# The order of VectorE's side work in a streamed-weight decoder layer: sums, prepared blocks and low parts issued behind the weights' low parts

## The chip, the cores and the metric

One core of a Trainium2 chip. The metric is device time in microseconds (us) of one launch; lower is better. In the profile PE is TensorE, DVE VectorE, ACT ScalarE, POOL GpSimd and SP SyncE, which issues nearly all transfers.

## The reference

One decoder layer on x of 256 tokens and 2048 channels, in float32: three residual blocks, each behind an RMSNorm, and a last RMSNorm.

```python
def swiglu(x, w_gate, w_up, w_down):
    return (jax.nn.silu(x @ w_gate) * (x @ w_up)) @ w_down

x = x + 0.5 * swiglu(rmsnorm(x), ...)                 # D_FF 5632
x = x + mixer(rmsnorm(x))                             # w_in: q,k,v,u,v_sg and two gates, 2048 wide each
x = x + 0.5 * swiglu(rmsnorm(x), ...)
out = rmsnorm(x)
```

The mixer projects once by `w_in`, runs dilated causal attention and a spatial gating unit beside each other, projects both to 2048 channels, merges them by sigmoid gates of `w_in`'s last columns and projects the merge by `w_out`.

## The kernel before

**Weights.** With 256 tokens all weights are used once, so they are streamed. A *unit* is a weight block of 2 x 128 rows by 512 columns. SyncE loads it into one of five buffers `raw` (`load_unit`, L206). Products must keep float32 accuracy, so each block is split: ScalarE rounds it to the high part `wh` (L281), VectorE subtracts for the low part `wl` (L282). Both live in a ring of nine slots of 128 rows. TensorE then makes three products for each slot and each of two token tiles, high x high, high x low and low x high (L288). One such ordinary step ("n") has twelve matmuls. The activations are split likewise: `xhi`/`xlo` for the block's normed input, `hA`/`hB` for the FFN's inner product (L380, L381).

**Quads.** Two neighbouring column groups of a product share a 2 x 2 arrangement of weight blocks (b11, b21, b12, b22) that is multiplied with seven products in place of eight (Strassen's method in Winograd's form). The products, `p1` to `p7`, are steps of their own ("s") of two or three slots, nine matmuls in a quad of three. VectorE prepares their weights from the blocks: t2 = b12 - b11, t1 = t2 - b22, t4 = b21 - t2 and, where the transfer doesn't add them up, b12 + b22 (`prepare`, L257 and L260). In the FFNs b12 + b22 is made by a second, accumulating load, which GpSimd issues once SyncE's load of b12 has landed (L247). VectorE also makes four sums of the activation blocks (`sums_of`, L360 to L363), which are split again into `fx`/`fh`. p1, p6 and p7 run among the last steps of the group before ("opening"), p5, p4, p3 and p2 among the first steps of their own ("closing": 1, 2, 4 and 6 ordinary steps in, where there are more than nine of them). Between them the partial results are copied or added between banks: after p1 and p7 a copy on ScalarE (L338, L343), after p6 one into `part` (L341), after p7 VectorE takes p7's result off `part` (L345), and after p5 it writes q12, a sum of p5's bank and `part` (L347), on which p3 then accumulates. A quad's blocks are loaded again for the next quad as they come free; the first quad of each home (FFN 1, gates, FFN 2) is loaded by `move_in`.

**Order.** The program is written out step by step, and each engine runs its instructions in the order in which they are written. For each step: its matmuls (`products`), then all callbacks that are due (a heap with due times counted in steps), then `advance`, which loads units and writes the splits of steps further on, three steps and up to two more if the ring has room. Quads' blocks are prepared at fixed steps beside p6: b12 + b22 three before, t2 two before, t1 two behind, t4 five behind, each just ahead of that step's split. So VectorE's and ScalarE's queues hold, between weight splits, the readings of banks directly behind the product, sums and low parts of activations when their callbacks come due, and prepared blocks at their fixed steps.

**Norms.** After each residual add (L471) ScalarE squares the sum (L437), VectorE and GpSimd make the reciprocal root (L441, L442, L444), and x is transposed through memory: VectorE writes `btx` (L408), SyncE stores it as `bmx` (L392) and reads it back as `xt` (L398), and some steps later (`lag`) ScalarE scales it by the gains (L490) and it is split. The FFN's product goes the same way.

Of the kernel before, what the change touches and what calls it, by code (L numbers as in the profile page):

```python
# [10 lines left out]
F32 = mybir.dt.float32  # L11
# [13 lines left out]
NC = 512  # L25
# [20 lines left out]
MORE = 7  # L46
UK = 4


@with_exitstack  # L50
def layer(ctx: ExitStack, tc: tile.TileContext, a, out):
    nc = tc.nc
    PE, ACT, DVE, POOL, SP = nc.tensor, nc.scalar, nc.vector, nc.gpsimd, nc.sync
    big = ctx.enter_context(tc.tile_pool(name="big", bufs=1))
# [54 lines left out]
    quads = []  # L109
    prepared = {}  # L110
    ends = []
# [16 lines left out]
    def lay_out():  # L128
        i, count = 0, 0
        while i < len(gemms):  # L130
            g = gemms[i]
            size, stage = g["group"]
            quad = g["quad"]
            taken = range(quad["k0"] // 2, quad["k0"] // 2 + quad["nq"]) if quad else ()
            order = [(p, q) for p in range(size) for q in range(gemms[i + p]["nk"] // 2) if q not in taken]
            if stage:
                order.sort(key=lambda s: stage(*s, gemms[i + s[0]]["nk"] // 2))
            new = [("n", (gemms[i + p], q // 2, q % 2)) for p, q in order]
            if quad:
                nq = quad["nq"]  # L140
                quad["gemms"] = gemms[i], gemms[i + 1]
                for k, form in opening(count):
# [42 lines left out]
    def at(i, fn):  # L185
        heapq.heappush(callbacks, (i, next(counter), fn))

    def start_of(w):
# [53 lines left out]
    def load_block(quad, b):  # L242
        if quad is None:
            return
        SP.dma_start(blocks_of(quad)[b], block(quad, b))
        if b == 2 and quad["home"] in homes:
            POOL.dma_start(blocks_of(quad)[b], block(quad, 3), accum_op=OP.add)  # L247
# [5 lines left out]
    def prepare(quad, what):  # L253
        b11, b21, b12, b22, t2, t1, _ = blocks_of(quad)
        if what == "t3":
            if quad["home"] not in homes:
                DVE.tensor_tensor(b12, b12, b22, op=OP.add)  # L257
            return
        out, x, y = {"t1": (t1, t2, b22), "t2": (t2, b12, b11), "t4": (t2, b21, t2)}[what]
        DVE.tensor_tensor(out, x, y, op=OP.subtract)  # L260

# [8 lines left out]

    now = [0.0]

    def split(i, k=None):
        for quad, what in prepared.pop(i, []):
            prepare(quad, what)
        kind, s = steps[i]
        r = raws[place[i]] if kind == "n" else form_of(*s)
        for first, end in runs(i, k or range(len(slots[i]))):
            o = slots[i][first]
            wh, wl = (v[:, o:o + end - first] for v in ring)  # L280
            ACT.activation(wh, r[:, first:end], AF.Copy)  # L281
            DVE.tensor_tensor(wl, r[:, first:end], wh.bitcast(F32), op=OP.subtract)  # L282
        if kind == "s" and s[1] in FREES:
            at(now[0] + 2, lambda: load_block(next_of(s[0]), FREES[s[1]]))

# [32 lines left out]
    def quad_products(i, quad, form):  # L318
# [17 lines left out]
        part = blocks_of(quad)[-1]  # L336
        if form == "p1":
            ACT.activation(q11, x_, AF.Copy)  # L338
            first["begun"][0] = True
        elif form == "p6":  # L340
            ACT.activation(part, x_, AF.Copy)  # L341
        elif form == "p7":
            ACT.activation(q21, x_, AF.Copy)  # L343
            first["begun"][1] = True
            DVE.tensor_tensor(part, part, x_, op=OP.subtract)  # L345
        elif form == "p5":
            DVE.tensor_tensor(q12, x_, part, op=OP.add)  # L347
            second["begun"][0] = True
        close(g, i)

    def sums_of(i, keep, q0, nq, store, v, name, tag="gate"):

        got = {}

        def sums():
# [6 lines left out]
            DVE.tensor_tensor(s3, a1, a0, op=OP.subtract)  # L362
            DVE.tensor_tensor(s4, b0, s2, op=OP.subtract)  # L363

        def parts():
            keep["both"] = both = store()
            split_psum(*both, got["f"])
# [10 lines left out]

    def split_psum(hi, lo, src):
        ACT.activation(hi, src, AF.Copy)  # L380
        DVE.tensor_tensor(lo, src, hi.bitcast(F32), op=OP.subtract)  # L381

# [83 lines left out]
    def residual(e, n, c, banks, scale, norm):  # L466
        cs = slice(c * NC, (c + 1) * NC)

        def add():
# [3 lines left out]
            if norm:  # L473
                if c == 0:
                    norm_open(n)
                norm_squares(n, c)

        at(e + 1, add)
        if not norm:
            return  # L480
        if c == 3:
            at(e + 2, lambda: norm_rstd(n))

        turn_x(e + (6 if c == 1 else 2), n, c, 6)

    def turn_x(i, n, c, lag, read=3):
        def evac(src):
# [3 lines left out]
            hi, lo = (turned(xT[p][:, 4 * c:4 * c + 4]) for p in ("hi", "lo"))  # L491
            split_psum(hi, lo, src)
            tag = "gate" if n == 1 else "tmp"
# [14 lines left out]
    def ffn(wg, wu, wd, down_post, group):  # L508
# [10 lines left out]
        for after, (part, quads_of) in zip(GATES, enumerate(PARTS)):  # L519
            for f in range(*after):  # L520
# [13 lines left out]
                def post_up(e, banks, st=st, f=f, kl=kl, quads_here=quads_here):  # L534
# [11 lines left out]
                    def ev(src):  # L546
                        hi, lo = (v[:, kl:kl + 4] for v in home["h"])
                        split_psum(turned(hi), turned(lo), src)
                        if first == 0:
                            st["fs"] = sb.tile([P, 2, 4, 3, P], F32R, tag="L", name=f"fh{e}")  # L550
                            sums_of(e + 10, st, 0, 2, lambda: [st["fs"][:, h, :, 0:2] for h in range(2)], src, f"h{e}")
                        elif first == 1 and quads_here["nq"] == 3:
                            sums_of(e + 10, st, 2, 1, lambda: [st["fs"][:, h, :, 2:3] for h in range(2)], src, f"h{e}")

# [598 lines left out]
    for i in range(n):  # L1153
# [10 lines left out]
        if i > 0:  # L1164
            advance(i)
    for t in range(NT):
        known(t)
# [52 lines left out]
```

## Time and profile before

| | us |
|---|---|
| three runs | 2029.78, 2031.58, 2035.73; median 2031.58 |
| the profiled execution | 2030.45 |
| its span | 2028.7 |
| TensorE busy | 1987.0 (98%) |
| VectorE busy | 1585.5 (78%) |
| ScalarE busy | 1177.8 (58%) |

The profile lists, for each engine, how long it waited, for which other engine's instruction and how often; the timeline shows single instructions with start, duration and, in brackets, the idle time ahead of them and what ended it. The first FFN runs from the start to about 670 us, the mixer from there to about 1360, the second FFN to the end.

### The profile page before, as it was taken

To read this page: it belongs to the slowest core of one execution; us is meant where nothing else is said; L and a number is where in the kernel's file an instruction comes from. 1 tells how busy PE (TensorE), PEld (TensorE's weight loads), DVE (VectorE), ACT (ScalarE), POOL (GpSimd) and SP (SyncE) were. 2 spreads that over 40 slices of the span, in tenths; PEclk is the share of its full clock that TensorE was granted. 3 is DMA by queue.
4 is the path that set the end of the run, shared out by engine and by line. 5 is a ranking of instruction groups with operands and counts; after the bars stand their busy time and mean duration, and the time that the engine had idled before them with its cause. 6 is when DMAs were issued, how large, how long until landed. Compare 5 with 4: busy or idle time off the path is not lost.

```text
span 2028.7 us, 25057 instructions
## 1 busy us (share of the span) xinstructions
PE 1987.0 (98%) x9188; PEld 1723.7 (85%) x9188; DVE 1585.5 (78%) x1652; ACT 1177.8 (58%) x1381; POOL 51.4 (3%) x50
## 2 busy tenths in 40 slices
PE   9999999999999999999999999989999999999998
PEld 8878888888888878888888888878888888888887
DVE  6788888887897689676665777787888878888876
ACT  7565555665665566455454555565665565655564
POOL 0000000000000000000000000000000000000000
PEclk9999999999999999999999999999999999999999
DMA  9888878877777985888887766788778877888783
GB/s 318 264 239 264 257 231 243 274 229 250 246 234 231 279 268 180 232 291 254 264 242 242 216 206 219 221 260 246 242 233 263 254 231 235 252 240 253 241 271 125
DMA packets 265445, 493.91 MB, mean 243 GB/s; under 512 B 17517, under 2 KB 46057, under 8 KB 265193
## 3 DMA queue, kind: packets, MB, share of 16 engines
q1 hardware_dynamic: 253624, 469.49, 71.9%
q0 software_dynamic: 11376, 22.28, 6.2%
q8 instruction: 72, 1.18, 0.2%
q10 hardware_dynamic: 320, 0.53, 0.1%
q14 instruction: 53, 0.43, 0.1%
HBM read 462.58 MB, written 29.66 MB: 243 GB/s over the span
## 4 chain that ended last, share of the span: by engine, by line
PE 75%; DVE 10%; DMA 6%; issue 4%; ACT 3%; SPq 1%; DVEq 0%; ACTq 0%; POOLq 0%; POOL 0%
PE qd L288 52%; PE mm L288 22%; DVE wl L282 6%; DMA xt<-bmx 2%; ACT wh L281 1%; DMA raw<-in_ffn_w_gate_dram 1%; DVE quads L260 1%; SPq L398 1%; DMA bmx<-btx 1%; DMA quads<-in_ffn_w_gate_dram 1%; ACT xt L490 1%; DVE sum L260 0%; DVE hB L381 0%; ACT xhi L380 0%; DVE btx L408 0%
## 5 line engine op out<-in xcount | busy, mean ns | idle before, releaser
L282 DVE TENSOR_TENSOR wl<-raw,wh 128x1024 fp32r<-128x1024 f32 (+1 forms) x638 | 695.4, 1107 | 202.1 <-ACT wh L281 200.7
L281 ACT ACTIVATE wh<-raw 128x1024 fp32r<-128x1024 f32 (+1 forms) x638 | 599.6, 961 | 312.2 <-PE qd L288 152.5
L288 PE MATMUL qd<-wl,xhi 128*128 128x512 f32 x1201 | 457.7, 381 | 8.9 <-DVE wl L282 8.9
L288 PE MATMUL qd<-wh,xhi 128*128 128x512 f32 x1201 | 456.7, 380 | 3.8 <-ACT wh L281 3.8
L288 PE MATMUL qd<-wh,xlo 128*128 128x512 f32 x1201 | 456.7, 380 | 0.0
L282 DVE TENSOR_TENSOR wl<-quads,wh 128x1536 fp32r<-128x1536 f32 (+2 forms) x223 | 290.9, 1317 | 94.4 <-ACT wh L281 93.1
L281 ACT ACTIVATE wh<-quads 128x1536 fp32r<-128x1536 f32 (+2 forms) x223 | 249.0, 1127 | 174.6 <-PE qd L288 153.2
L288 PEld LDWEIGHTS qd<-wl,xhi 128*128 128x128 f32 x1201 | 227.6, 190 | 44.7 <-DVE wl L282 12.4
L288 PEld LDWEIGHTS qd<-wh,xhi 128*128 128x128 f32 x1201 | 227.6, 189 | 37.4 <-ACT wh L281 5.0
L288 PEld LDWEIGHTS qd<-wh,xlo 128*128 128x128 f32 x1201 | 227.8, 190 | 32.2
L288 PE MATMUL mm<-wh,xhi 128*128 128x512 f32 x608 | 231.7, 381 | 0.4 <-ACT xhi L380 0.2
L288 PE MATMUL mm<-wh,xlo 128*128 128x512 f32 x608 | 230.9, 380 | 0.6 <-DVE xlo L381 0.6
L288 PE MATMUL mm<-wl,xhi 128*128 128x512 f32 x608 | 229.4, 380 | 0.1
L288 PE MATMUL qd<-wl,hA 128*128 128x512 f32 x564 | 214.1, 380 | 1.8 <-DVE wl L282 1.8
L288 PE MATMUL qd<-wh,hA 128*128 128x512 f32 x564 | 213.8, 379 | 0.0
L288 PE MATMUL qd<-wh,hB 128*128 128x512 f32 x564 | 213.8, 379 | 0.0
L282 DVE TENSOR_TENSOR wl<-sum,wh 128x1024 fp32r<-128x1024 f32 (+2 forms) x85 | 117.8, 1393 | 64.0 <-ACT wh L281 64.0
L288 PEld LDWEIGHTS mm<-wl,xhi 128*128 128x128 f32 x608 | 115.2, 189 | 18.0 <-DVE wl L282 1.9
L288 PEld LDWEIGHTS mm<-wh,xlo 128*128 128x128 f32 x608 | 115.2, 189 | 17.4 <-DVE xlo L381 1.0
L288 PEld LDWEIGHTS mm<-wh,xhi 128*128 128x128 f32 x608 | 115.2, 189 | 17.1 <-ACT xhi L380 0.6
L288 PE MATMUL qd<-wh,fx 128*128 128x512 f32 x352 | 120.2, 382 | 4.3 <-ACT wh L281 4.0
L281 ACT ACTIVATE wh<-sum 128x1024 fp32r<-128x1024 f32 (+2 forms) x85 | 100.7, 1191 | 38.3 <-PE qd L288 26.6
(453 smaller groups left out, 2192.1 us busy)
## 6 DMA issues: line engine op xcount, KB each, us to landing
raw<-in_w_in_dram SPq DMA_DIRECT2D x168, 512.0 KB, 4.8
raw<-in_ffn_w_down_dram SPq DMA_DIRECT2D x120, 512.0 KB, 5.0
raw<-in_ffn_w_up_dram SPq DMA_DIRECT2D x112, 512.0 KB, 6.1
raw<-in_ffn_w_gate_dram SPq DMA_DIRECT2D x111, 512.0 KB, 4.1
quads<-in_ffn_w_gate_dram SPq DMA_DIRECT2D x38, 768.0 KB, 5.3
quads<-in_ffn_w_up_dram SPq DMA_DIRECT2D x38, 768.0 KB, 5.9
quads<-in_ffn_w_down_dram SPq DMA_DIRECT2D x32, 512.0 KB, 6.0
quads<-in_ffn_w_up_dram POOLq DMA_DIRECT2D x19, 768.0 KB, 11.1
```

Of the source, the lines that this page charges most:

```text
L260: DVE.tensor_tensor(out, x, y, op=OP.subtract)
L281: ACT.activation(wh, r[:, first:end], AF.Copy)
L282: DVE.tensor_tensor(wl, r[:, first:end], wh.bitcast(F32), op=OP.subtract)
L288: PE.matmul(g["ps"][t], act, in_turn(w), start=not g["begun"][t], stop=g["left"][t] == 0, skip_group_check=g["quad"] is not None)
L398: SP.dma_start(e[32 * j:32 * j + 32].rearrange("p (i r) -> p i r", i=4), m[j])
L490: ACT.activation(v, v, AF.Copy, scale=g)
```

## The change

- `Metered` stands in for VectorE when instructions are written. It books 0.03 us plus a microsecond per 950 columns for each in `load`; at each step's end `work_off` takes 2.6 off per ordinary step.
- Low parts of activations and the four sums may be handed to `extra` with a slack. `work_off` writes them at the end of a step, behind its weight splits, if they are ready and `load` with them stays within 2.9, or if their slack has run out. hB gets 4 steps, the sums of h 5, those of x 1; xlo of mixer and second FFN comes one step later, except the last block's. The sums' split follows two steps behind the sums (one for x) and not one.
- Quads' blocks are no longer prepared at fixed steps. `prepare_ready` takes the next (b12 + b22, t2, t1, t4) at a step's end if the blocks' loads were issued three steps ago or more, the product that still needs the old contents has been split, and `load` allows; `prepare_for` writes it at the latest ahead of the split that uses it.
- Readings of banks (p1, p6, p7, p5) are gathered in `after_splits` and written behind the step's splits.
- The closing order is p5, p3, p4, p2 at 1, 2, 3 and 5 ordinary steps (short groups: 1, 2, 3, 4).
- The block that p5 frees is loaded one step later and not two; squares are made three steps behind the add and not one, the root four and not two; the last transposed block is scaled seven steps after its transpose and not six; the first blocks of the gates' and the second FFN's quads are loaded 4 and 2 steps later.

No instruction is added or removed on TensorE, VectorE, ScalarE or SyncE; some instructions only change place. The core of the diff:

```diff
+TICK = 2.6
+FULL = 2.9
+class Metered:
+        def call(out, *args, **kwargs):
...
+            self.load += 0.03 + columns / 950
+            return method(out, *args, **kwargs)
...
     def closing(count):
-        return zip((1, 2, 4, 6) if count > 9 else (1, 2, 3, 5), ("p5", "p4", "p3", "p2"))
+        return zip((1, 2, 3, 5) if count > 9 else (1, 2, 3, 4), ("p5", "p3", "p4", "p2"))
...
+    def work_off():
+        DVE.load = max(0.0, DVE.load - TICK * (now[0] - now[1]))
+        now[1] = now[0]
+        while True:
+            ready = [e for e in extras if e[2] <= now[0]]
+            if not ready:
+                return
+            e = min(ready)
+            if e[0] > now[0] and DVE.load + e[3] > FULL:
+                return
...
+            e[4]()
...
+    NEEDS = {"f": ((2, 3), ()), "t2": ((0, 2), ("p1",)), "t1": ((3,), ("p1",)), "t4": ((1,), ("p6",))}
+    USES = {"p6": "t2", "p7": "f", "p5": "t1", "p4": "t4"}
+    def prepare_ready():
...
+            if (all(quad["loaded"].get(b, 1e9) + 3 <= now[0] for b in blocks) and quad["split"].issuperset(forms)
+                    and DVE.load + 0.56 * quad["nq"] * (NC / 512) <= FULL):
...
+                prepare_next(quad)
...
-            at(now[0] + 2, lambda: load_block(next_of(s[0]), FREES[s[1]]))
+            at(now[0] + (1 if s[1] == "p5" else 2), lambda: load_block(next_of(s[0]), FREES[s[1]]))
...
+        after_splits.append(read)
...
-        at(i, sums)
-        at(i + 1, parts)
+        at(i + 1, lambda: extra(0, slack, 0.6 + 0.6 * nq, sums) if slack > 1 else sums())
...
+        if slack:
+            extra(1, slack, 1.1, rest)
+        else:
+            rest()
...
-        turn_x(e + (6 if c == 1 else 2), n, c, 6)
+        at(e + 3, lambda: norm_squares(n, c))
         if c == 3:
-            at(e + 2, lambda: norm_rstd(n))
+            at(e + 4, lambda: norm_rstd(n))
+        turn_x(e + (6 if c == 1 else 2), n, c, 7 if c == 3 else 6)
...
-    for after, home in ((16, homes[0]), (mixer + 1, gates), (start_of(ffn2_gate) + 1, homes[1])):
+    for after, home in ((16, homes[0]), (mixer + 5, gates), (start_of(ffn2_gate) + 3, homes[1])):
...
-    for i, (kind, s) in enumerate(steps):
-        if kind == "s" and s[1] == "p6":
-            for k, what in ((-3, "t3"), (-2, "t2"), (2, "t1"), (5, "t4")):
-                prepared.setdefault(i + k, []).append((s[0], what))
...
         if i > 0:
             advance(i)
+        for fn in after_splits:
+            fn()
+        after_splits.clear()
+        work_off()
+        prepare_ready()
```

How it moves the instructions, at three places. First VectorE around p5 of the first FFN's first quad (97 to 108 us in the trace). `sg` is the gate's activation times the up product, `fsh` the four sums of h, `fh` their split, `wl<-sum` and `wl<-quads` low parts of a quad's block, `qd_2` the q12 sum. Before:

```order
L381 TENSOR_TENSOR hB<-sg19.0_583,hA 128x1024
L360 TENSOR_TENSOR fsh23.0_847<-sg19.0_583 128x256
L361 TENSOR_TENSOR fsh23.0_847<-sg19.0_583,fsh23.0_847 128x256
L362 TENSOR_TENSOR fsh23.0_847<-sg19.0_583 128x256
L363 TENSOR_TENSOR fsh23.0_847<-sg19.0_583,fsh23.0_847 128x256
L381 TENSOR_TENSOR fh23.0_846<-fsh23.0_847,fh23.0_846 128x4x256
L543 SCALAR_TENSOR_TENSOR sg27.75_738<-mm_0_291,rstd_443,sg27.75_738 128x512
L543 SCALAR_TENSOR_TENSOR sg27.75_738<-mm_1_292,rstd_443,sg27.75_738 128x512
L282 TENSOR_TENSOR wl<-sum,wh 128x512
L282 TENSOR_TENSOR wl<-sum,wh 128x1024
L347 TENSOR_TENSOR qd_2_706<-qd_3_707,quads 128x512
L282 TENSOR_TENSOR wl<-raw_739,wh 128x1024
```

After (all VectorE instructions bear L66, the line in `Metered`):

```order
L66 SCALAR_TENSOR_TENSOR sg27.75_740<-mm_0_291,rstd_440,sg27.75_740 128x512
L66 SCALAR_TENSOR_TENSOR sg27.75_740<-mm_1_292,rstd_440,sg27.75_740 128x512
L66 TENSOR_TENSOR wl<-quads,wh 128x512
L66 TENSOR_TENSOR wl<-quads,wh 128x1024
L66 TENSOR_TENSOR hB<-sg19.0_583,hA 128x1024
L66 TENSOR_TENSOR wl<-raw_741,wh 128x1024
L66 TENSOR_TENSOR qd_2_707<-qd_3_708,quads 128x512
L66 TENSOR_TENSOR fsh23.0_880<-sg19.0_583 128x256
L66 TENSOR_TENSOR fsh23.0_880<-sg19.0_583,fsh23.0_880 128x256
L66 TENSOR_TENSOR fsh23.0_880<-sg19.0_583 128x256
L66 TENSOR_TENSOR fsh23.0_880<-sg19.0_583,fsh23.0_880 128x256
```

hB and the sums went behind a quad's low part, the sums behind the q12 sum as well, the q12 sum behind one more `wl<-raw`, and the low part ahead of it is now p3's (`quads`) and no longer p4's (`sum`). fh's split stands five low parts further down.

Second, SyncE at the start of the second FFN (1352 to 1370 us). Before:

```order
L206 DMA raw_9768<-in_ffn_w_up_dram 128x2x512
L245 DMA quads<-in_ffn_w_gate_dram 128x3x512
L245 DMA quads<-in_ffn_w_up_dram 128x3x512 x2
L245 DMA quads<-in_ffn_w_gate_dram 128x3x512
L206 DMA raw_9813<-in_ffn_w_up_dram 128x2x512
L392 DMA bmx_3_9837<-btx_3_9834 128x1024
```

After:

```order
L250 DMA raw_9764<-in_ffn_w_up_dram 128x2x512
L250 DMA raw_9795<-in_ffn_w_up_dram 128x2x512
L468 DMA bmx_3_9815<-btx_3_9812 128x1024
L290 DMA quads<-in_ffn_w_gate_dram 128x3x512
L290 DMA quads<-in_ffn_w_up_dram 128x3x512 x2
L290 DMA quads<-in_ffn_w_gate_dram 128x3x512
```

The four loads of the first quad stand behind one unit and behind the store of the last transposed block.

Third, VectorE at the same place (1371 to 1388 us): `wl<-quads` is p1's low part, `sum<-quads` t2, `quads<-sum,quads` t1, `wl<-sum` p6's low part. Before:

```order
L282 TENSOR_TENSOR wl<-quads,wh 128x1536
L260 TENSOR_TENSOR sum<-quads 128x1536
L282 TENSOR_TENSOR wl<-raw_9813,wh 128x512 x2
L381 TENSOR_TENSOR xlo_9404<-xt_3_9881,xhi_9403 128x1024
L282 TENSOR_TENSOR wl<-raw_9839,wh 128x1024
L282 TENSOR_TENSOR wl<-sum,wh 128x1536
```

After:

```order
L66 TENSOR_TENSOR wl<-quads,wh 128x1536
L66 TENSOR_TENSOR sum<-quads 128x1536
L66 TENSOR_TENSOR wl<-raw_9795,wh 128x512 x2
L66 TENSOR_TENSOR wl<-raw_9838,wh 128x1024
L66 TENSOR_TENSOR quads<-sum,quads 128x1536
L66 TENSOR_TENSOR xlo_9400<-xt_3_9885,xhi_9399 128x1024
L66 TENSOR_TENSOR wl<-sum,wh 128x1536
```

t2 keeps its place behind p1's low part; t1 has come ahead of p6's, and the last xlo went behind one more low part and t1.

More of the change, by code (lines that the diff above doesn't have):

```diff
@@ L47, with __init__, __getattr__ @@
 UK = 4
+TICK = 2.6
+FULL = 2.9
+class Metered:
+    def __init__(self, engine):
+        self.engine, self.load = engine, 0.0
+    def __getattr__(self, name):
+        method = getattr(self.engine, name)
+        def call(out, *args, **kwargs):
+            columns = 1
+            for n in out.shape[1:]:
+                columns *= n
+            self.load += 0.03 + columns / 950
+            return method(out, *args, **kwargs)
+        return call
 @with_exitstack
@@ L52, in layer @@
     nc = tc.nc
-    PE, ACT, DVE, POOL, SP = nc.tensor, nc.scalar, nc.vector, nc.gpsimd, nc.sync
+    PE, ACT, DVE, POOL, SP = nc.tensor, nc.scalar, Metered(nc.vector), nc.gpsimd, nc.sync
     big = ctx.enter_context(tc.tile_pool(name="big", bufs=1))
@@ L109, in layer @@
     quads = []
-    prepared = {}
     ends = []
@@ L141, in lay_out @@
                 quad["gemms"] = gemms[i], gemms[i + 1]
+                quad["loaded"], quad["split"] = {}, set()
+                quad["todo"] = ["t2", "t1", "t4"] if quad["home"] in homes else ["f", "t2", "t1", "t4"]
                 for k, form in opening(count):
@@ L186, in at, with extra @@
         heapq.heappush(callbacks, (i, next(counter), fn))
+    now = [0.0, 0.0]
+    extras = []
+    after_splits = []
+    def extra(wait, slack, cost, fn):
+        heapq.heappush(extras, (now[0] + slack, next(counter), now[0] + wait, cost, fn))
+    def work_off():
[8 more added lines that the diff above has]
+                return
+            extras.remove(e)
+            heapq.heapify(extras)
+            e[4]()
     def start_of(w):
@@ L244, in load_block @@
             return
+        quad["loaded"][b] = now[0]
         SP.dma_start(blocks_of(quad)[b], block(quad, b))
@@ L254, in prepare, with prepare_next, prepare_for @@
         b11, b21, b12, b22, t2, t1, _ = blocks_of(quad)
[L255 to L260, printed above, removed]
+        out, x, y, op = {"f": (b12, b12, b22, OP.add), "t1": (t1, t2, b22, OP.subtract),
+                         "t2": (t2, b12, b11, OP.subtract), "t4": (t2, b21, t2, OP.subtract)}[what]
+        DVE.tensor_tensor(out, x, y, op=op)
+    NEEDS = {"f": ((2, 3), ()), "t2": ((0, 2), ("p1",)), "t1": ((3,), ("p1",)), "t4": ((1,), ("p6",))}
+    USES = {"p6": "t2", "p7": "f", "p5": "t1", "p4": "t4"}
+    def prepare_next(quad):
+        prepare(quad, quad["todo"].pop(0))
+    def prepare_ready():
+        for quad in started:
+            if not quad["todo"]:
+                continue
+            what = quad["todo"][0]
+            blocks, forms = NEEDS[what]
+            if (all(quad["loaded"].get(b, 1e9) + 3 <= now[0] for b in blocks) and quad["split"].issuperset(forms)
+                    and DVE.load + 0.56 * quad["nq"] * (NC / 512) <= FULL):
+                assert all(b in quad["loaded"] for b in blocks)
+                prepare_next(quad)
+    def prepare_for(quad, form):
+        while USES.get(form) in quad["todo"]:
+            assert all(b in quad["loaded"] for b in NEEDS[quad["todo"][0]][0]), (form, quad["todo"])
+            prepare_next(quad)
+    started = []
     def form_of(quad, form):
@@ L269, in layer @@
     ring = [big.tile([P, RING, NC], F32R, name=name) for name in ("wh", "wl")]
-    now = [0.0]
     def split(i, k=None):
-        for quad, what in prepared.pop(i, []):
-            prepare(quad, what)
         kind, s = steps[i]
+        if kind == "s":
+            if s[1] == "p1":
+                started.append(s[0])
+            prepare_for(*s)
+            s[0]["split"].add(s[1])
         r = raws[place[i]] if kind == "n" else form_of(*s)
@@ L336, in quad_products, with read, sums_of @@
         part = blocks_of(quad)[-1]
[L337 to L348, printed above, removed]
+        def read():
+            if form == "p1":
+                ACT.activation(q11, x_, AF.Copy)
+            elif form == "p6":
+                ACT.activation(part, x_, AF.Copy)
+            elif form == "p7":
+                ACT.activation(q21, x_, AF.Copy)
+                DVE.tensor_tensor(part, part, x_, op=OP.subtract)
+            elif form == "p5":
+                DVE.tensor_tensor(q12, x_, part, op=OP.add)
+        after_splits.append(read)
+        if form in ("p1", "p7", "p5"):
+            (second if form == "p5" else first)["begun"][form == "p7"] = True
         close(g, i)
-    def sums_of(i, keep, q0, nq, store, v, name, tag="gate"):
+    def sums_of(i, keep, q0, nq, store, v, name, tag="gate", slack=1):
         got = {}
@@ L363, in sums @@
             DVE.tensor_tensor(s4, b0, s2, op=OP.subtract)
+            at(now[0] + min(2, slack), parts)
         def parts():
             keep["both"] = both = store()
-            split_psum(*both, got["f"])
+            split_psum(*both, got["f"], slack // 2)
             keep.setdefault("forms", {}).update({q0 + q: [v[:, :, q] for v in both] for q in range(nq)})
-        at(i, sums)
-        at(i + 1, parts)
+        at(i + 1, lambda: extra(0, slack, 0.6 + 0.6 * nq, sums) if slack > 1 else sums())
     def forms_tile(pool, tag, name, nq):
@@ L491, in evac @@
             hi, lo = (turned(xT[p][:, 4 * c:4 * c + 4]) for p in ("hi", "lo"))
-            split_psum(hi, lo, src)
+            split_psum(hi, lo, src, 1 if n and c < 3 else 0)
             tag = "gate" if n == 1 else "tmp"
@@ L547, in ev @@
                         hi, lo = (v[:, kl:kl + 4] for v in home["h"])
[L548 removed]
+                        split_psum(turned(hi), turned(lo), src, 0 if last else 4)
                         if first == 0:
                             st["fs"] = sb.tile([P, 2, 4, 3, P], F32R, tag="L", name=f"fh{e}")
[L551 removed]
+                            sums_of(e + 10, st, 0, 2, lambda: [st["fs"][:, h, :, 0:2] for h in range(2)], src, f"h{e}", slack=5)
                         elif first == 1 and quads_here["nq"] == 3:
[L553 removed]
+                            sums_of(e + 10, st, 2, 1, lambda: [st["fs"][:, h, :, 2:3] for h in range(2)], src, f"h{e}", slack=5)
                     at(e + 1, mul)
```

6 lines of the change are left out of this document (3 added, 3 removed).

## The prediction

> **What bounds the kernel now.** I read the page first, then TensorE's waits, the same waits by window, and the timelines around the longest of them. The page:
>
> ```profile
> span 2028.7 us, 25057 instructions
> PE 1987.0 (98%) x9188; PEld 1723.7 (85%) x9188; DVE 1585.5 (78%) x1652; ACT 1177.8 (58%) x1381; POOL 51.4 (3%) x50
> ```
>
> TensorE bounds it: it is busy 1987.0 of 2028.7 us, and the change leaves its work as it is. Only its stops can be won. TensorE's waits over the whole span, the two rows that matter (sum, times, longest):
>
> ```profile
> PE qd L288 <- DVE wl L282: 22.9, 26, 2.1
> PE qd L288 <- ACT wh L281: 7.7, 10, 1.8
> ```
>
> 36 stops, 30.6 us, all for the low or high part of a weight block. Where they lie: the same view for 20 to 640 us (first FFN), 640 to 720 (its end and the mixer's start), 1280 to 1400 (the mixer's end and the second FFN's start) and 1400 to 2020 (second FFN), in this order:
>
> ```profile
> PE qd L288 <- DVE wl L282: 6.4, 7, 1.9
> PE qd L288 <- ACT wh L281: 1.4, 3, 0.8
> ```
> ```profile
> PE qd L288 <- DVE wl L282: 3.9, 4, 2.1
> PE qd L288 <- ACT wh L281: 1.2, 1, 1.2
> ```
> ```profile
> PE qd L288 <- DVE wl L282: 6.6, 8, 1.7
> PE qd L288 <- ACT wh L281: 2.6, 2, 1.8
> ```
> ```profile
> PE qd L288 <- DVE wl L282: 5.3, 6, 1.3
> PE qd L288 <- ACT wh L281: 2.5, 4, 1.2
> ```
>
> A stop costs more than its idle time. TensorE's timeline at the longest of the first FFN (six rows left out between 107.12 and 110.19):
>
> ```profile
> 103.67 0.38 PE L288 MATMUL qd<-wh,xhi 128*128 128x512 f32 x1
> 105.98 0.48 PE L288 MATMUL qd<-wl,xhi 128*128 128x512 f32 x1 [1.93 <-DVE wl L282]
> ...
> 107.12 0.72 PE L288 MATMUL qd<-wl,xhi 128*128 128x512 f32 x1 [0.22 <-DVE wl L282]
> ...
> 110.19 0.60 PE L288 MATMUL qd<-wh,xlo 128*128 128x512 f32 x1
> 110.62 0.39 PE L288 MATMUL qd<-wh,xhi 128*128 128x512 f32 x1
> ```
>
> And TensorE undisturbed (one row left out between the first two), at the end of a product p5, with VectorE's work on that bank behind it:
>
> ```profile
> 1145.55 0.38 PE L288 MATMUL qd<-wh,uTB 128*128 128x512 f32 x1
> ...
> 1145.99 0.38 PE L288 MATMUL qd<-wh,uTA 128*128 128x512 f32 x1
> 1146.20 0.38 PE L288 MATMUL qd<-wh,xhi 128*128 128x512 f32 x1
> ```
> ```profile
> 1147.37 0.70 DVE L347 TENSOR_TENSOR qd<-qd,part 128x512 f32<-128x512 f32 x1
> 1147.97 1.22 DVE L282 TENSOR_TENSOR wl<-raw,wh 128x1024 fp32r<-128x1024 f32 x1
> ```
>
> Starts lie 0.65/3 = 0.217 us apart, so twelve matmuls, one ordinary step, take 2.60 us. A stop loses the overlap of the last matmul's end (0.38 - 0.217 = 0.16) and makes the next one longer (0.48 for 0.38): 0.26 beside its idle time. From 107.12 to 110.62 eight matmuls take 3.50 us where 1.73 are usual: a clock drop, 1.77 lost. I count three such drops: here, at 715 (one matmul's row below) and behind the stop at 1384, shown further down. Everything that the stops cost is 30.6 idle + 36 x 0.26 (9.4) + 3 x 1.77 (5.3) = 45 us.
>
> What VectorE did ahead of the stop at 105.98, in its timeline (from the start of an activation's low part to the weights' that TensorE wants):
>
> ```profile
> 98.97 1.22 DVE L381 TENSOR_TENSOR hB<-sg19.0_583,hA 128x1024 fp32r<-128x1024 f32 x1
> 100.11 0.42 DVE L360 TENSOR_TENSOR fsh23.0_847<-sg19.0_583 128x256 f32<-128x256 f32 x1
> ...
> 102.78 1.23 DVE L381 TENSOR_TENSOR fh23.0_846<-fsh23.0_847,fh23.0_846 128x1024 fp32r<-128x1024 f32 x1 [1.12 <-ACT fh23.0_846 L380]
> ...
> 105.24 1.82 DVE L282 TENSOR_TENSOR wl<-sum,wh 128x512 fp32r<-128x512 f32 x2
> ```
>
> From 98.97 to 104.0 it makes nothing that TensorE needs soon, and 1.12 of it is spent waiting for ScalarE. The same sums hold ScalarE's queue in a later group:
>
> ```profile
> 134.30 0.63 ACT L380 ACTIVATE fh23.0_846<-fsh33.25_1060 128x512 fp32r<-128x512 f32 x1 [2.79 <-DVE fsh33.25_1060 L363]
> ```
>
> Behind it stands the next weight's high part. So both rows of the table have the same cause: work without hurry ahead of weights.
>
> **The change part by part.** The sum is made on the profiled execution, 2030.45 us (its span 2028.7 and 1.75 around), 1.1 under the median of the three runs.
>
> *Sums, hB and fh split behind weights, two steps apart.* The low part, the sums and their split cost the same as before (no instruction added or removed), but stand behind the step's weights and are let out only when the account has room. In the two FFNs this concerns 6.4 + 1.4 + 5.3 + 2.5 = 15.6 us idle in 20 stops, 20 x 0.26 = 5.2, and the drop at 107 (1.8): 22.6. I take 20 of it as gone; bounds 12 and 22.6. What hides the moved work is VectorE's idle fifth; its users come four or more steps later.
>
> *Mixer's start.* ScalarE scales a transposed block that comes late, and the first quad's high part stands behind it. ScalarE, VectorE (two rows, an earlier block and this one), TensorE:
>
> ```profile
> 707.79 1.71 ACT L490 ACTIVATE xt<-xt,gcols 128x256 f32<-128x256 f32 x4 [5.75 <-DMA xt<-bmx]
> ```
> ```profile
> 690.91 1.23 DVE L381 TENSOR_TENSOR xlo<-xt,xhi 128x1024 fp32r<-128x1024 f32 x1 [1.46 <-ACT xhi L380]
> ...
> 710.62 1.23 DVE L381 TENSOR_TENSOR xlo<-xt,xhi 128x1024 fp32r<-128x1024 f32 x1 [7.32 <-ACT xhi L380]
> ```
> ```profile
> 711.59 0.48 PE L288 MATMUL qd<-wh,xhi 128*128 128x512 f32 x1 [1.22 <-ACT wh L281]
> 714.17 0.48 PE L288 MATMUL qd<-wl,xhi 128*128 128x512 f32 x1 [2.10 <-DVE wl L282]
> ...
> 715.46 0.63 PE L288 MATMUL qd<-wh,xlo 128*128 128x512 f32 x1
> ```
>
> With a step more of lag (2.60) the quad's high and low part stand ahead of that wait: 1.22 + 2.10 + 2 x 0.26 + 1.77 = 5.6 gone; the window's other 5.1 - 3.3 = 1.8 us of stops, behind squares that ScalarE made ahead of weights, go with 0.2 left: -2. Against that, the earlier blocks' xlo goes behind two weights' low parts (1.13 each, by the step from 1147.97's kind of row, 1.22 less the overlap), and its user is close: one or two stops of 1 to 2.3 us, with 0.26 and perhaps a drop each, 4 in all (0 to 7). Net -4.
>
> TensorE's clock fell at 107 after stops of 1.93 and 0.22 us, so I price a stop of 2 us or more with 1.77. [...]
>
> *Second FFN's start.* SyncE, TensorE, VectorE, and the page's row of the accumulating loads:
>
> ```profile
> 1356.12 0.41 SPq L245 DMA_DIRECT2D quads<-in_ffn_w_gate_dram  x1
> ...
> 1365.85 0.34 SPq L392 DMA_DIRECT2D bmx<-btx  x1
> ```
> ```profile
> 1384.59 0.48 PE L288 MATMUL qd<-wh,xhi 128*128 128x512 f32 x1 [1.80 <-ACT wh L281]
> ```
> ```profile
> 1375.68 1.76 DVE L260 TENSOR_TENSOR sum<-quads 128x1536 f32<-128x1536 f32 x1 [0.60 <-DMA quads<-in_ffn_w_up_dram]
> ```
> ```profile
> quads<-in_ffn_w_up_dram POOLq DMA_DIRECT2D x19, 768.0 KB, 11.1
> ```
>
> The first blocks now stand behind bmx on SyncE, and SyncE reaches bmx only when VectorE has written it. Even with that write a step earlier (1363), the loads start 7 us later than at 1356.12. The sum t2 waited for the accumulated block already (0.60), 19.6 after the first load; from 1363 that is 1382.6, and VectorE stands there some 7 us with the weights' low parts of three steps behind it. TensorE has about two steps (5.2) in hand: a stop of 2 to 5 us and a drop, 5.5 in all. What goes is that 1.80 with its 0.26, a drop of 1.77 and a smaller stop behind it, about 5; the window's other stops I leave as they are. Net +1 (-4 to +6).
>
> [...]
>
> *The q12 sum.* Before, the sum after p5 (L347) was issued as soon as p5 was, and its result first needed by p3 after p4 and three ordinary steps. Now p3 follows p5 after one step, and the sum stands behind that step's low part. p5's end at 1145.99 + 0.38 = 1146.37; the sum ended at 1148.07; with the low part ahead (its step 1.13) at 1149.20, 2.83 after p5. p3 would start 2.60 - 0.16 = 2.44 after it: 0.39 late, with 0.10 for the longer first matmul 0.5. A three-wide group of the FFN stands better:
>
> ```profile
> 1647.84 0.38 PE L288 MATMUL qd<-wh,fy 128*128 128x512 f32 x1
> ```
> ```profile
> 1649.00 0.69 DVE L347 TENSOR_TENSOR qd<-qd,quads 128x512 f32<-128x512 f32 x1
> ```
>
> 1649.69 + 1.13 is 2.60 after p5's end at 1648.22: 0.16 late, 0.26 in all, and nothing where VectorE is less behind now. There are 38 quads (the 38 block loads a column in the page agree): 22 at 0.26, 14 at 0.5 and two in the mixer at about 2 would be 17. Since the work moved away leaves VectorE earlier at these places, I take 12, with 3 and 26 as bounds.
>
> *t2, t1, t4 by the account.* They may come a step earlier than their accumulated load allows elsewhere too: +2 (0 to 5). p5's reload a step earlier and rstd later have cover of several steps: 0.
>
> Sum: 2030.45 - 20 - 4 + 1 + 12 + 2 = 2021.
>
> **The rivals.** *The q12 sum decides, slower.* If at p5's end VectorE is half a low part further back than at 1146 (0.56), each p3 comes 0.95 late, 1.05 with the longer matmul, 38 x 1.05 = 40 in place of 12: 2049. It makes the kernel slower than the median's 2031.6 from (10.6 + 12)/38 = 0.59 per quad on. For: VectorE is 78% busy, and the sum at 1649.00 starts 0.78 after p5 with no wait of its own. Against: what delayed it is what the account takes away.
>
> *Nearly all stops go.* If the account keeps VectorE within a step of TensorE everywhere, q12 costs 3 and the starts of mixer and second FFN nothing new: 2030.45 - 22.6 - 8 - 4 + 3 = 1999. Against it stands the wait for the transfer at 1375.68, which no account knows of.
>
> *The stops only change place.* VectorE's work is the same 1585.5 us; what is put off comes due at its deadline in the same dense steps. Then 12 of 20 go and the q12 sums take 12 and more: about 2030.
>
> **How the numbers follow.** Forecast case 0.62 (its own range 2008 to 2028), nearly all 0.12, change of place 0.16, slower by q12 0.10. A measurement can tell 0.3%, 6.1 us, from no change: faster is below 2025.5, slower above 2037.7. Of the forecast case nine tenths lie below 2025.5: faster 0.57 + 0.12 = 0.69, same 0.16 + 0.05 = 0.21, slower 0.10. The range for 8 in 10 takes the nearly-all case in part and change of place wholly: 2001 to 2034.
>
> **What would show it.** Right: TensorE's stops in 20 to 640 and 1400 to 2020 fall from 15.6 to under 6 us, the waits for sums ahead of ScalarE's high parts go, and short waits of TensorE for the q12 sum (0.1 to 0.5 each) appear in their place; a VectorE wait of several us for the accumulated block near 1375 to 1385; no stop at 711. Wrong: p3's waits sum to more than 20 us, or TensorE's waits for low parts in the FFNs stay above 10, or no new wait at the second FFN's start.

## The result and the profile after

The changed kernel takes 2015.92 us (median of four, 2014.04 to 2018.70); the kernel before, in the runs beside it, 2032.44 (2029.78 to 2035.73). The ratio is 0.9919, with a 95% interval of 0.9898 to 0.994: some 16.5 us less, where 9.4 were forecast (2021 for 2030.45). The profiled execution of the changed kernel is the slowest of its four, 2018.70, with a span of 2017.0, so its trace shows 11.7 of the 16.5.

Its page, first lines:

```profile
span 2017.0 us, 25183 instructions
PE 1984.2 (98%) x9188; PEld 1726.5 (86%) x9188; DVE 1589.4 (79%) x1652; ACT 1189.0 (59%) x1381; POOL 57.1 (3%) x50
```

The engines do what they did (TensorE 1987.0 and 1984.2, VectorE 1585.5 and 1589.4); only stops went. TensorE's waits over the span (sum, times, longest), where before two rows held 30.6 us:

```profile
PE qd L355 <- DVE qd L66: 6.3, 6, 3.8
PE mm L355 <- DVE xlo L66: 4.9, 1, 4.9
PE qd L355 <- DVE wl L66: 4.3, 3, 3.2
PE qd L355 <- ACT qd L407: 2.3, 1, 2.3
```

Waits for weights' low parts fell from 22.9 us to 5.6 (4.3 in the quads' banks `qd`, 1.3 in a row of `mm` banks left out here), and those for high parts are gone. In their place stand waits for the q12 sum (`DVE qd`), for xlo and one for a bank copied by ScalarE.

Waits leave out what a stop costs beside its idle time (before, 15.6 us of waits from 20 to 640 and 1400 to 2020, against 23.1 lost in the shorter stretches below), so the FFNs are better read by matmuls in a fixed stretch. The view by windows of the two kernels, 60 to 640 and 1430 to 1960 us, TensorE's busy time and matmuls in the third and fourth column; before, then after:

```profile
60.00:640.00 580.00, 572.10 (x2631) 497.13 (x2630) 479.12 (x453) 339.60 (x370) 22.51 (x21) 1.00 0.80 248
1430.00:1960.00 530.00, 522.12 (x2408) 454.16 (x2407) 446.91 (x418) 315.00 (x338) 17.75 (x14) 1.00 0.80 247
```
```profile
60.00:640.00 580.00, 578.50 (x2675) 504.48 (x2674) 490.07 (x465) 351.43 (x380) 27.81 (x21) 1.00 0.81 249
1430.00:1960.00 530.00, 529.56 (x2451) 462.44 (x2450) 453.51 (x426) 321.65 (x341) 17.75 (x14) 1.00 0.82 252
```

A kernel shown below runs 2689 and 2457 there without one stop: 580/2689 = 0.2157 us a matmul. Before, 58 and 49 are missing, 12.5 and 10.6 us; after, 14 and 6, 3.0 and 1.3. So the FFNs gave 9.5 + 9.3 = 18.8 us, and the rest of the layer took some 7 back in this trace. The longest new stops stand at three places. At the mixer's start, TensorE and VectorE:

```profile
678.94 0.38 PE L355 MATMUL mm<-wl,xhi 128*128 128x512 f32 x1
684.20 0.80 PE L355 MATMUL mm<-wh,xlo 128*128 128x512 f32 x1 [4.88 <-DVE xlo L66]
```
```profile
679.47 1.23 DVE L66 TENSOR_TENSOR wl<-raw,wh 128x1024 fp32r<-128x1024 f32 x1 [3.03 <-ACT wh L348]
681.78 1.23 DVE L66 TENSOR_TENSOR wl<-raw,wh 128x1024 fp32r<-128x1024 f32 x1 [1.09 <-ACT wh L348]
682.92 1.22 DVE L66 TENSOR_TENSOR xlo<-xt,xhi 128x1024 fp32r<-128x1024 f32 x1
```

xlo stands behind two low parts, as the order showed; but these waited themselves, 3.03 and 1.09 us, for ScalarE. Among the mixer's strips VectorE is full (busy 21.7 of the 22.0 us from 750 to 772), the q12 sum comes last, and p3 waits:

```profile
771.70 0.69 DVE L66 TENSOR_TENSOR qd<-qd,vs 128x512 f32<-128x512 f32 x1
```
```profile
772.54 0.77 PE L355 MATMUL qd<-wh,fx 128*128 128x512 f32 x1 [3.80 <-DVE qd L66]
```

And at the second FFN's start t2 waits for the accumulated block, with a low part that TensorE needs behind it:

```profile
1377.31 1.76 DVE L66 TENSOR_TENSOR sum<-quads 128x1536 f32<-128x1536 f32 x1 [6.12 <-DMA quads<-in_ffn_w_up_dram]
```
```profile
1379.72 0.74 PE L355 MATMUL qd<-wl,xhi 128*128 128x512 f32 x1 [3.21 <-DVE wl L66]
```

Behind the three stops 13, 6 and 7 matmuls start 0.43 us apart in place of 0.217; the trace's granted clock is 0.50, 0.50 and 0.51 there.

### The profile page after: what moved, and what is told of

Read it like the earlier page. It is cut to its first block, busy times and chain, and to the rows that moved or that the text cites. A ratio compares the mean times of both kernels' runs of the same rounds, so it can differ in the third digit from the quotient of the medians.

```text
span 2017.0 us, 25183 instructions
## 1 busy us (share of the span) xinstructions
PE 1984.2 (98%) x9188; PEld 1726.5 (86%) x9188; DVE 1589.4 (79%) x1652; ACT 1189.0 (59%) x1381; POOL 57.1 (3%) x50
## 4 chain that ended last, share of the span: by engine, by line
PE 86%; DVE 5%; DMA 4%; issue 2%; ACT 2%; SPq 0%; POOLq 0%; POOL 0%; ACTq 0%; DVEq 0%
PE qd L355 65%; PE mm L355 20%; DVE wl L66 3%; DMA raw<-in_w_in_dram 1%; DMA raw<-in_ffn_w_gate_dram 1%; ACT wh L348 1%; DMA raw<-in_ffn_w_up_dram 1%; DMA quads<-in_ffn_w_up_dram 0%; DMA bmu<-btu 0%; DVE vs L66 0%; DVE quads L66 0%; DVE sum L66 0%; ACT xt L566 0%; DMA xt<-bmx 0%; PE sp L802 0%
## 5 line engine op out<-in xcount | busy, mean ns | idle before, releaser
L66 DVE TENSOR_TENSOR wl<-raw,wh 128x1024 fp32r<-128x1024 f32 (+1 forms) x638 | 695.2, 1107 | 227.0 <-ACT wh L348 224.2
L348 ACT ACTIVATE wh<-raw 128x1024 fp32r<-128x1024 f32 (+1 forms) x638 | 609.0, 963 | 414.8 <-PE qd L355 236.9
L66 DVE TENSOR_TENSOR wl<-quads,wh 128x1536 fp32r<-128x1536 f32 (+2 forms) x222 | 289.6, 1319 | 142.6 <-ACT wh L348 141.6
L66 DVE TENSOR_TENSOR wl<-sum,wh 128x1024 fp32r<-128x1024 f32 (+2 forms) x86 | 117.5, 1375 | 10.3 <-ACT wh L348 10.3
```

Source lines behind the costliest of these rows:

```text
L66: return method(out, *args, **kwargs)
```

## The experiments

The theory: hB, the sums and their split, standing ahead of weights, made the stops in the FFNs, and the near use of q12, the deferred xlo and the late first blocks took part of the gain back. The rivals put the gain elsewhere (readings, prepared blocks, the closing order) or the new stops down to other causes. "Of before" is the ratio to the kernel before on the same chip, with its 95% interval.

**Only the sums.** hB, sums and their split as changed; the rest taken back (closing order, `prepared` at its fixed steps, `read()` at once, squares, xlo, lag, first blocks, p5's reload):

```diff
-        after_splits.append(read)
+        read()
...
-        prepare_ready()
...
-        return zip((1, 2, 3, 5) if count > 9 else (1, 2, 3, 4), ("p5", "p3", "p4", "p2"))
+        return zip((1, 2, 4, 6) if count > 9 else (1, 2, 3, 5), ("p5", "p4", "p3", "p2"))
```

> Of the change only the account for hB, the sums of h and x and their split (issued behind the weights' splits, with slack, the split two steps later); closing order, fixed steps of prepared blocks, readings of banks, squares, xlo, lag and first blocks as before. Theory (hB, sums and their split made the stops in the FFNs): TensorE's waits in 20 to 640 and 1400 to 2020 fall from 15.6 us to under 5, those at 711 and 1384 stay; 12 to 20 us less than before, ratio 0.990 to 0.994, about as the whole change. Rival (prepared blocks at fixed steps and bank readings ahead of splits are the larger part): waits in the FFNs stay above 9 us and the time is within 8 us of before.

2014.11 us, 0.9901 of before (0.9886 to 0.9915). The same windows:

```profile
60.00:640.00 580.00, 578.05 (x2674) 504.41 (x2672) 486.11 (x462) 345.61 (x381) 23.19 (x21) 1.00 0.81 249
1430.00:1960.00 530.00, 527.72 (x2440) 460.36 (x2439) 449.36 (x420) 317.29 (x340) 17.75 (x14) 1.00 0.82 251
```

15 and 17 matmuls are missing in place of 58 and 49, and the FFNs' waits are 3.9 us in place of 15.6. The sums alone give the time of the whole change: everything else, added to them, comes out at nothing together.

**The sums without the account's limit.**

```diff
-FULL = 2.9
+FULL = 100.0
```

> The kernel with the sums alone (hB, sums of h and x and their split put behind the weights' splits, all else as before the change), and the account's limit raised to 100, so that each is written at the first step's end at which it is ready. Theory (their place behind the weights' splits is what counts, and two steps between the sums and their split): equal to the kernel with the sums alone within 2 us, 0.990 to 0.992 of before. Rival (the account, which puts them into a step with room, is what counts): waits for low parts in the FFNs come back to 8 us or more, 6 to 14 us slower than with the account.

2013.98 us, 0.9898 (0.9885 to 0.9911): as with the limit. So the account's limit is not what counts for the sums. The place behind the step's splits and the longer distance between sums and split are left; they were not tried apart. No run shows a gain from the limit.

**All but the sums.** In the changed kernel hB, the sums of h and their split are written when due:

```diff
-                        split_psum(turned(hi), turned(lo), src, 0 if last else 4)
+                        split_psum(turned(hi), turned(lo), src)
...
-                            sums_of(e + 10, st, 0, 2, lambda: [st["fs"][:, h, :, 0:2] for h in range(2)], src, f"h{e}", slack=5)
+                            sums_of(e + 10, st, 0, 2, lambda: [st["fs"][:, h, :, 0:2] for h in range(2)], src, f"h{e}")
```

> The changed kernel with hB, the sums of h and their split taken out of the account: written when due, ahead of the step's weights' splits, the sums one step later than before the change, their split one step behind them. All else of the change stays. Theory (these three make the stops in the FFNs): TensorE's waits for low and high parts in 20 to 640 and 1400 to 2020 come back to 8 us or more, and the time is 8 to 16 us above the changed kernel. Rival (the readings behind the splits and the blocks by the account give VectorE the room, whatever the sums do): waits there stay under 4 us and the time is within 3 us of the changed kernel.

2019.42 us, 0.9929 (0.9916 to 0.9942); beside it on the same chip the changed kernel itself:

> The changed kernel as it is, on the same chip as the three beside it, so that they can be set against it. Both theories: 0.989 to 0.994 of before; waits for a q12 sum at 768 (3.8 us) and of 4.9 us for xlo at 679 again.

2019.71 us, 0.9925 (0.9911 to 0.9939). The theory falls in its simple form. TensorE's waits of the kernel without the moved sums from 20 to 640 us:

```profile
PE qd L355 <- DVE qd L66: 1.7, 2, 1.6
```

Not one wait for a weight's part is left, though hB and the sums stand ahead of weights again; from 1400 to 2020 it is the same (1.2 us, for q12 sums). The rival was right, and something else in the change removes the same stops. Two runs ask which.

**Only the prepared blocks by the account.** `prepare_ready` and `prepare_for` as changed, all else as before.

> Of the change only the quads' blocks prepared by the account; sums, hB, readings, closing order and all else as before. Theory as it now stands (the stops in the FFNs come where hB, sums and a prepared block of 1.67 us fall into the same steps; taking either away clears them): FFN waits fall from 15.6 to under 5 us, 0.989 to 0.994 of before. Rival (readings behind the splits made the difference in the run without the account for sums): FFN waits stay above 10 us, within 6 us of before.

2032.37 us, 0.9987 (0.9978 to 0.9996): the theory as it stood then falls as well, and its rival holds (14.4 us of waits in the FFNs); 61 and 56 matmuls are missing:

```profile
60.00:640.00 580.00, 573.13 (x2628) 496.24 (x2627) 479.46 (x454) 340.26 (x371) 21.65 (x21) 1.00 0.80 247
1430.00:1960.00 530.00, 522.05 (x2401) 452.29 (x2400) 446.72 (x418) 315.95 (x338) 17.75 (x14) 1.00 0.79 246
```

**Only the readings behind the splits.** The four readings of banks are gathered in `after_splits`, all else as before.

> Of the change only the readings of banks behind the step's splits; all else as before. Theory: a reading is 0.6 us, a third of a prepared block, so it moves little: FFN waits stay above 9 us, within 6 us of before. Rival (readings waited for the product's end with weights' low parts queued behind them, so they were the large part): FFN waits under 5 us, 0.989 to 0.994 of before.

2019.06 us, 0.9923 (0.991 to 0.9935): 15.5 us for a move that I had held to be small. The two windows:

```profile
60.00:640.00 580.00, 574.44 (x2650) 499.63 (x2649) 485.15 (x459) 344.64 (x373) 23.29 (x21) 1.00 0.81 248
1430.00:1960.00 530.00, 525.60 (x2426) 457.70 (x2426) 448.93 (x417) 317.20 (x337) 17.75 (x14) 1.00 0.82 251
```

39 and 31 matmuls are missing in place of 58 and 49, so the FFNs gave 4.1 + 3.9 = 8.0 us of it, and the rest lies outside them. The theory was right that the FFNs' waits stay above 9 us (10.9), the rival on the time. But the waits are others: those for weights' parts fell from 15.6 to 1.0 us. ScalarE's waits in the kernel before, three rows of copies, fit that:

```profile
ACT qd L343 <- PE qd L288: 74.4, 34, 3.3
ACT qd L338 <- PE qd L288: 65.7, 35, 3.5
ACT quads L341 <- PE qd L288: 39.6, 31, 3.9
```

A copy of a bank waits for the product's last matmul, and the step's high parts stand behind it: in 100 places, 179.7 us in all, ScalarE could not work ahead. With the readings behind the splits, these rows are gone; ScalarE's first row in this kernel is its wait for the product that frees a ring slot:

```profile
ACT wh L348 <- PE qd L355: 472.2, 423, 2.6
```

That wait was 335.0 us before: ScalarE now waits when it is further ahead. That ScalarE, and VectorE behind it, so come to the sums with a lead is my reading of these rows. VectorE's own two readings hardly waited for a product in the kernel before (0.2 us), but they were not moved apart from ScalarE's. What is left in the FFNs is mostly new: waits of up to 1.6 us for copies that come too late behind sums and splits (3.9 and 5.0 us in the two FFNs). The row of the first:

```profile
PE qd L355 <- ACT quads L409: 3.9, 3, 1.6
```

**Sums, prepared blocks and readings together**, without the closing order, squares, xlo, lag, first blocks and p5's reload:

> Sums, prepared blocks by the account and readings behind the splits as changed; closing order, p5's reload, squares, rstd, lag, xlo and first blocks as before. Theory (prepared blocks and readings only clear the small stops that sums alone leave in the FFNs, 0.4 to 0.9 us each, 4 us in all, and may bring the near waits at the merges): FFN waits under 2 us, 2 to 5 us less than with the sums alone, 0.987 to 0.990. Rival (they cost as much at 1280 to 1400 as they save in the FFNs): equal to the sums alone within 2 us, waits of over 8 us between 1280 and 1400.

2005.67 us, 0.9858 (0.9845 to 0.9872), the fastest of all: 14 us under the changed kernel on the same chip, and by the ratios 9 under the sums alone, where 2 to 5 were expected. In both windows the FFNs run without a stop:

```profile
60.00:640.00 580.00, 580.00 (x2689) 507.88 (x2688) 491.60 (x468) 351.77 (x383) 22.08 (x21) 1.00 0.82 250
1430.00:1960.00 530.00, 530.00 (x2457) 463.76 (x2456) 454.15 (x426) 322.73 (x347) 16.47 (x13) 1.00 0.82 252
```

**The same with the new closing order.**

```diff
-        return zip((1, 2, 4, 6) if count > 9 else (1, 2, 3, 5), ("p5", "p4", "p3", "p2"))
+        return zip((1, 2, 3, 5) if count > 9 else (1, 2, 3, 4), ("p5", "p3", "p4", "p2"))
```

> The kernel with sums, prepared blocks and readings as changed, and with the new closing order as well. Theory (the nearer use of q12 costs the stops that the changed kernel shows: 3.8 us and a drop at 768, 1 to 2 us at 1354, 0.85 at 1978, against 1.67 and 0.98 at 756 to 762 with the old order): 3 to 6 us slower than without it, 0.987 to 0.989 of before. Rival (all 38 sums late): over 15 us slower. Second rival (the order costs nothing, since stops at the mixer's end only change their name): equal within 2 us.

2017.95 us, 0.9918 (0.9905 to 0.9932): 0.0060 of 2034.5 more, 12.2 us, from some 7 to 18 by the ends of the two intervals. More than the 3 to 6 expected, and about as much as separates the fastest version from the changed kernel. TensorE's waits from 640 to 800 and from 1280 to 1400:

```profile
PE qd L355 <- DVE qd L66: 6.6, 2, 3.8
```
```profile
PE qd L355 <- DVE ms L66: 5.0, 1, 5.0
PE qd L355 <- DVE qd L66: 2.0, 1, 2.0
```

The `ms` row is a q12 sum too: it ran from 1359.29 to 1359.98, the instruction ahead of `ms`, and p3 began at 1360.13. The four stops of 2 us and more begin at 637, 770, 1307 and 1355. Within the FFNs the order costs less: 2666 matmuls in the first window, 23 missing, 5.0 us, half of it the stop at 637; 2451 in the second, 6 missing, 1.3 us.

**The changed kernel with the old closing order:**

> The changed kernel with the old closing order (p5, p4, p3, p2 at 1, 2, 4, 6). Theory (the nearer use of the q12 sum costs what the trace shows, 6.3 us idle in 6 stops, 3.8 of it at 768.7 with a clock drop of 1.77): 6 to 9 us less than the changed kernel, no wait for a q12 sum left. Rival (the closing order frees blocks and prepared sums earlier and carries part of the gain): p4's sum t4 comes due sooner again and waits for low parts come back in the FFNs; equal to the changed kernel or up to 10 us slower.

2014.33 us, 0.9902 (0.9888 to 0.9917), against 0.9919 and 0.9925 of the changed kernel. The intervals overlap, so by itself this run settles nothing. The q12 waits are gone, but the stop at the second FFN's start is 4.60 in place of 3.21, and there is one of 3.65 for xlo at 1355. Beside the fastest version the run says more. The two differ by p5's reload, squares, root, lag, xlo and first blocks alone, and by 0.0044, 9 us, with intervals that lie apart. So these parts together cost 9 us with the old closing order and nothing with the new (0.9918 without them, 0.9919 and 0.9925 with them): the losses, too, do not add up.

**xlo at once.**

```diff
-            split_psum(hi, lo, src, 1 if n and c < 3 else 0)
+            split_psum(hi, lo, src, 0)
```

> The changed kernel with one edit: the low part xlo of the mixer's and the second FFN's blocks is written at once and not a step later. Theory (the deferral makes the 4.88 us stop at 679): xhi was ready at 678.5 and VectorE stood idle from 676.4 to 679.5, so xlo would end near 680.2; TensorE's stop there falls to 1 to 2 us and its clock drop (1.77) may go; 3 to 6 us less than the changed kernel, ratio to before 0.989 to 0.991. Rival (the late unit is the cause: ScalarE waited 4.00 us for a raw load ahead of xt): the stop stays at 4 us or more, wherever xlo stands, and the time is that of the changed kernel within 2 us.

2017.76 us, 0.9921 (0.9908 to 0.9935): as the changed kernel. Neither side had it right: the stop at 679 is gone, and one of 4.18 us stands at 698. ScalarE and TensorE there:

```profile
698.44 1.70 ACT L566 ACTIVATE xt<-xt,gcols 128x256 f32<-128x256 f32 x4 [7.12 <-DMA xt<-bmx]
```
```profile
702.23 0.80 PE L355 MATMUL mm<-wh,xhi 128*128 128x512 f32 x1 [4.18 <-ACT wh L348]
```

The stop has passed to the next thing that is late, the last transposed block. Its bmx store began at 679.98 here and at 676.46 in the changed kernel; what moved it was not tried.

**The second FFN's first blocks two steps earlier.**

```diff
-(start_of(ffn2_gate) + 3, homes[1])
+(start_of(ffn2_gate) + 1, homes[1])
```

> The changed kernel with the second FFN's first blocks loaded at the old step (2 steps earlier). Theory: the loads start ahead of the store bmx, some 5 us earlier, VectorE's wait of 6.12 us for the accumulated block at 1377 falls under 1.5, TensorE's stop of 3.21 at 1376.5 and its clock drop go: 4 to 6 us less. Rival (the blocks collide with the transposed block's way through memory): xt comes back later and ScalarE's wait for it stops TensorE as in the kernel before (1.8 and 1.0 us, and a drop); within 2 us of the changed kernel.

2014.62 us, 0.99 (0.9885 to 0.9915). By the times alone unclear; by the trace as the theory says: VectorE's wait for the block is 0.3 us in place of 6.12, TensorE waits nowhere from 1360 to 1420:

```profile
DVE sum L66 <- DMA quads<-in_ffn_w_up_dram: 0.3, 1, 0.3
```

**Squares and root later, added to the fastest version.**

> The kernel with sums, prepared blocks and readings as changed, and with the squares three steps and the root four steps behind the add as well. Theory (at the end of the first FFN ScalarE's squares and VectorE's add stand ahead of the weights and make the 3.58 us stop at 652): that stop falls under 1 us, 3 to 5 us less than without it, 0.982 to 0.985 of before. Rival (a later root and later squares hold back the last transposed block): the stop comes back at 680 to 700 with 3 to 5 us, and the time is equal.

2007.76 us, 0.9867 (0.9854 to 0.9881): no gain. The stop at 652 stays, 3.53 us for 3.58, so squares did not make it; a stop of 3.32 comes at 1367 as well. In the fastest version's trace VectorE's sums of x wait there for a store to read the buffer that they write into:

```profile
652.95 0.43 DVE L66 TENSOR_TENSOR fsx<-xt 128x256 f32<-128x256 f32 x1 [3.52 <-DMA bmx<-btx]
```

That this wait makes the stop is read from the trace and was not tried.

## Why the prediction was right, point by point

**TensorE's stops are all there is to win:** right. Its work stayed, and the best version gained by stops alone.

**The signs:** most came. The FFNs' waits fell to 2.4 us, no stop is left at 711, and VectorE waits 6.12 us for the accumulated block. The waits for q12 came, but as 6 with one of 3.8 us, not as many of 0.1 to 0.5.

**The FFNs' 22.6 us, 20 of them gone:** right in size, and a little low. Without the closing order all 12.5 + 10.6 = 23.1 us in the two windows went; the changed kernel keeps 18.8 of them, or 17.7 with a stop for q12 at 1978. The forecast left the FFNs some 14 to 16 (20 less about 4 of the 12 for q12 and up to 2 for t2), 2 to 4 too little.

**Their cause:** the step that failed. I put all of it on "work without hurry ahead of weights", and priced the readings' move behind the splits only as a delay of q12. Moved alone, the readings gain 15.5 us, the sums alone 20, prepared blocks alone some 2 (4.5 at most by the interval), the three together 30. Of the FFNs' 15.6 us of waits for weights' parts the sums alone leave 3.9 and the readings alone 1.0, so the gains overlap and do not add up; the readings alone bring 8.9 us of waits for copies in their place. My reading is that these stops need both a burst of sums and engines that come to it without a lead, because the readings tie them to the product's end. That each move clears them is shown; the lead as the reason is argued from ScalarE's waits. There was a row for it, ScalarE's 179.7 us of waits in front of copies, in a view that I left out because ScalarE is idle 42% of the time.

**The q12 sum, 12 us (3 to 26):** the size was met in another kernel than the one forecast, which is in part luck. Added to the fastest version the closing order costs 12.2; taken back in the changed kernel it gives 3.5 to 4.7, not clear of noise, and the waits for q12 there are 6.3 us. I had it spread evenly, 5.7 of 17 in 22 FFN quads. Where it costs 12.2, the waits lie at four places (637, 770, 1307, 1355), 13.6 us in all and 2.0 to 5.0 each, and the granted clock is 0.98, 0.98 and 0.97 in the stretches 640 to 720, 720 to 800 and 1280 to 1400; some take the place of other stops. "Two in the mixer at about 2" was mis-sized.

**Mixer's start, -4:** wrong in size. The stop at 711 went, as said, and xlo's came, but at 4.88 us for the 1 to 2.3 forecast, since the low parts ahead of it waited for ScalarE, and with a drop of 2.8. By the same matmul in both traces, 640 to 720 gained 1.0 us. That placing xlo earlier moves the stop and doesn't remove it was not foreseen.

**Second FFN's start, +1:** right by its mechanism. t2 waited 6.12 us (forecast some 7), TensorE 3.21 (2 to 5) with a drop. The loads started at 1357.14 for 1356.12, while p1's low part there came at 1369.43 for 1373.33: 5 us later against the program, where I had taken 7.

**The clock, 1.77 a stop of 2 us or more:** a drop came at each of the three stops above, but of 2.8, 1.3 and 1.5 us by the matmuls 0.43 apart. A stop of 2.29 us had one in one execution and none in another, below, so a price by length alone does not hold here.

**The accumulated load:** GpSimd issued it at 1365.80, and VectorE was free from 1371.2. The wait ended at 1377.31, 11.5 us after the issue and 20.2 after the first load at 1357.14; the forecast's 19.6 from the first load to t2, taken from the trace of before, was close.

**The rivals.** "q12 decides" named a real cost and the wrong size: 12 where it cost most, not 40. "Nearly all stops go", a gain of 31 us, is near what the best version gains, 30, without the closing order and the smaller parts. "The stops only change place" is true outside the FFNs alone.

So the time lay in the range and 5 us under the forecast. By the same matmuls in the two traces the FFNs gave 17.7 us, 640 to 720 gave 1.0, and 720 to 1400 took 7.2: the FFNs gave 2 to 4 more than forecast and the mixer's start 3 less, errors that partly cancel. The traces differ by 11.7 us and the medians by 16.5; where the other 4.8 lie is open.

## What to carry to other kernels

Where an engine runs its instructions in the order written, as ScalarE did in the kernel before with 179.7 us of waits in front of copies, look at what waits for a late result ahead of work that is ready: such an instruction can hold the engine up even where it is idle 42% of the time. Putting it behind the ready work gained 15.5 us here, beside 20 for moving the work that is not urgent. A step that is brought nearer to its producer must be checked where the engine between them is fullest, not at the average place. And a change of many parts that gains 0.8% may hold one that costs 0.6% beside the good parts alone and hardly shows when only it is undone (0.2%): build up from the parts that gain, since neither gains nor losses that share a cause add up.

## What the runs showed of the hardware

A stop's length alone did not settle the clock drop here. The same stop of 2.29 us at the same place of the same program was followed by half clock in one execution and not in another; the changed kernel twice, each a stop and a matmul about 2 us behind it:

```profile
1334.68 0.48 PE L355 MATMUL qd<-wh,fx 128*128 128x512 f32 x1 [2.29 <-ACT qd L407]
...
1336.70 0.63 PE L355 MATMUL qd<-wh,mhi 128*128 128x512 f32 x1
```
```profile
1336.01 0.48 PE L355 MATMUL qd<-wh,fx 128*128 128x512 f32 x1 [2.29 <-ACT qd L407]
...
1338.06 0.38 PE L355 MATMUL qd<-wh,mhi 128*128 128x512 f32 x1
```

In the first the granted clock was 0.50 from 1335.50 to 1338.80, with matmuls 0.43 us apart; ten steps from one matmul's start to the next, from 1335.00 to 1338.83, took 3.83 us where 2.17 are usual. In the second they stayed 0.216 apart. The traces of the kernel before and of the changed kernel hold eight stops over 1.5 us. Those of 4.88, 3.80, 3.21, 2.29, 2.10, 1.93 and 1.80 us were followed by slow matmuls, the last two with a second stop of 0.22 and 0.96 us in between; the one of 1.73, at 1332.90 in the kernel before, was not: the clock was 1.00 in the 6 us from there.

So beside its idle time the stop of 2.29 us cost 1.7 us at half clock in one execution and none in the other. What decides it was not shown. Six executions of the changed kernel on one chip lie up to 8 us apart (2014.51 to 2022.16). The granted clocks of the fastest and the slowest, 0.996 and 0.994, make some 4 us of that by estimate (0.002 of 2018).
